# S5 tables of both layers in one opening pass, contiguous weights and a SwiGLU in two halves

## The chip, the cores and the metric

The kernel runs on one core of a Trainium2 chip. The metric is the device time of one execution in microseconds (us). The five engines work side by side, each through its own queue of instructions in program order: TensorE (PE, matmuls; PEld, its weight loads), VectorE (DVE), ScalarE (ACT), GpSimd (POOL) and SyncE (SP), which here issues most transfers. An instruction that waits for a semaphore holds up all that stand behind it on its engine.

## The reference

A trunk of two layers works on 512 tokens, 256 of context and 256 of the latent, of 1024 columns each, in float32. Each layer scales and shifts its input by modulations, projects it, runs four mixers (gated DeltaNet, S5, HGRN2, retention) over it, joins them by an output product with a residual and a layer norm, and ends with a SwiGLU: a dense one of 2816 columns in layer 0, eight experts of 3584 columns, two per token, in layer 1.

```python
for layer in range(DEPTH):
    mod_lat = jax.nn.silu(c) @ ada_w[layer] + ada_b[layer]
    sh1, sc1, gt1, sh2, sc2, gt2 = jnp.split(mod_lat[:, None, :], 6, axis=-1)
    p_lat = _split_proj(_f32((x * (1.0 + sc1) + sh1) @ w_in[layer]))
    ...
    x = _layer_norm(ALPHA * x + gt1 * (mix_lat @ w_out[layer]), ln_g[layer, 0], ln_b[layer, 0])
    # ffn: silu(h @ w1) * (h @ w3) @ w2, dense in layer 0, top 2 of 8 experts in layer 1
    x = _layer_norm(ALPHA * x + gt2 * ffn(x * (1.0 + sc2) + sh2), ln_g[layer, 1], ln_b[layer, 1])

# S5: a diagonal complex state space, per direction, group and state
lam_bar = jnp.exp(lam * jnp.exp(log_step)[..., None])
b_bar = ((lam_bar - 1.0) / lam)[..., None] * lax.complex(b_re, b_im)
h_t = lam_bar * h_(t-1) + b_bar u_t;  y_t = Re(c_mat h_t)
```

The context goes the same way with its own modulations (the last layer needs only the latent's).

## The kernel before

Every product in float32 is made of three matmuls on a high and a low half. `weight` (L340) has SyncE load a block as it is (`wraw`, L344), ACT casts the high half (`whi`, L348) and DVE subtracts the low one (`wlo`, through `tt` at L263). `stationary` and `product` then issue three matmuls of 512 columns per 128 rows (L331): hi with xh, hi with xl, lo with xh, into a PSUM bank `psacc`. A helper's line stands in the profile for all its uses, so tiles tell the stages apart.

`run` puts the stages in this order. (1) `ada` for the first two modulations of layer 0: 16 blocks of 512 KB (`sraw`, 12 buffers), two matmuls each, then a small product `psP`. (2) `first_input` loads the transposed tokens into the same `sraw` ring, scales them and splits them into xh and xl. (3) `mixers(0)`: projections in groups of 256 columns (`w_in`), S5, retention, gated DeltaNet, HGRN2. (4) `mixed`: the output product over the whole of `w_out`, with the residual. (5) `norm_feat`: the layer norm and the modulated input of the SwiGLU. (6) `ffn`: for each of 22 blocks of 128 columns the products with w1 and w3, SiLU times the gate (the multiplication on GpSimd), the high half on ACT and the low half `fgl` on GpSimd; then w2 over 8 output blocks with 22 rows each. (7) a norm that also keeps a transposed copy (`keep`), `mixers(1)`, the output product by tokens, and the experts: 8 experts x 7 steps x 6 units of 1 MB (`mraw`, 8 buffers, L1756).

`s5_tables(l)` prepares what S5 multiplies with. It begins with scalar columns (16 per layer: exponentials, powers of lambda, phases), which DVE and GpSimd compute. Then four groups follow, each with loads of B and C, complex products of 512 columns (`cmul`: the one for the input table `s5W` on DVE with `s5tmp`, the one for the output table on GpSimd with `s5tmq`), 8 transposes of `s5W`, products `s5cz` x `s5W` on TensorE, and writes to DRAM. At the end 16 products with `s5kfb` make a Toeplitz table. Layer 0's tables are called in `mixers(0)` after the first projections, layer 1's between `norm_feat` and `ada(1, ...)`, in a pool of their own.

What stands where on an engine is decided when the program is built: a scheduler lays the instructions of all stages out by priority and by its own estimate of when operands are ready. `prior(off)` and `high_priority(off)` shift a part's priority, contexts name which PSUM banks a part takes, and a pool that isn't left keeps its room. On the chip each engine then keeps that order.

Of the kernel before, what the change touches and what calls it, by code (L numbers as in the profile page):

```python
# [143 lines left out]

def input_arrays(x):
# [14 lines left out]
    for k in ("ada_w", "w_in", "w_out", "ln_g", "ln_b", "ffn_w1", "ffn_w3", "ffn_w2", "moe_w1", "moe_w3", "moe_w2"):  # L160
        arrays[k] = np.ascontiguousarray(g(k))
# [27 lines left out]
class Trunk:  # L189
# [101 lines left out]
    def exp(self, out, x):  # L291

        n = x.shape[1]
        k, r, p = (self.t("ex" + c, [16], bufs=2, pool=self.sc)[:, :n] for c in "krp")
        ki = self.t("exi", [16], I32, bufs=2, pool=self.sc)[:, :n]
# [42 lines left out]
    def weight(self, src, shape, hi_eng="act", lo_eng="vec", pool=None, raw_bufs=3, bufs=2, tag="w", raw=None):  # L338
# [52 lines left out]
    def ada(self, l, part, pool=None, tag="w", bufs=3):  # L391
# [25 lines left out]
    def first_input(self, pool, bufs):  # L417
# [6 lines left out]
        for k0 in range(0, KT, 2):  # L424
            raw = self.t("sraw", [2, NTOK], F32, bufs, pool)
# [17 lines left out]
    def stationary(self, w, xh, xl, acc, eng=("act", "vec")):  # L443

        K = w.shape[1]
        for k0 in range(0, K, 8):
            kn = min(8, K - k0)
            hi, lo = self.weight(w[:, k0:k0 + kn], [kn, P], *eng)
# [7 lines left out]
    def product(self, w, xh, xl, n, fn):  # L456

        for i in range(w.shape[2] // P):
            acc = self.ps("acc")[:, :n]
            self.stationary(w[:, :, i * P:(i + 1) * P], xh, xl, acc)  # L460
            fn(i, acc)

    @projecting
    def proj_feat(self, l, c0, fn, tok=(0, NTOK), ncol=256):

        w = self.A["w_in"][l].rearrange("(k p) f -> p k f", p=P)[:, :, c0:c0 + ncol]
        a, b = tok
# [422 lines left out]
    def gdn_proj(self, l, full):  # L890
# [11 lines left out]
        self.proj_few(l, C_GAB, 16, self.gab)  # L902
# [248 lines left out]
    def s5_tables(self, l):  # L1151
        nc, G = self.nc, self.G
        e = G
        v = lambda k: self.Pm(k).rearrange("p (l g) -> p l g", l=DEPTH)[:, l]
        n = lambda tag, *s: self.t("s5" + tag, list(s))
        self.load_consts("sconsts")
        are, aim = v("s5re"), v("s5im")
        st, ar, ai, t0, t1 = (n(x, 16) for x in ("st", "ar", "ai", "t0", "t1"))
        self.exp(st, v("s5ls"))
# [11 lines left out]
        U = n("u", 2, 16)  # L1171

        h2, sh, ch = (n(x, 16) for x in ("h2", "sh", "ch"))
# [23 lines left out]
        ltmp = n("lt", 16, 4)  # L1197
        pw = lambda a, b: (L[:, 0, :, a:b], L[:, 1, :, a:b])
        for m in (1, 2, 4):
            bc = tuple(x.to_broadcast([P, 16, m]) for x in pw(m, m + 1))  # L1200
            self.cmul(pw(m + 1, 2 * m + 1), pw(1, m + 1), bc, ltmp[:, :, :m])
        self.V.tensor_copy(res[:, 1552:1584].rearrange("p (c g) -> p c g", c=2), L[:, :, :, 8])

        q, nr, den = n("q", 2, 16), n("nr", 16), n("den", 16)
# [14 lines left out]
        LW, LC = n("LW", 2, 16, 8), n("LC", 2, 16, 8)  # L1219
# [13 lines left out]
        pr, pi = self.s5_phases(res)  # L1233
# [798 lines left out]
    def run(self):  # L2032
# [3 lines left out]
        for p in (0, 1):  # L2036
            self.ada(0, p, start, "s", bufs)
# [63 lines left out]
```

## Time and profile before

| | |
|---|---|
| Three runs | 2555.76, 2555.69, 2549.09 us (median 2555.69) |
| Profiled execution | 2555.49 us, span 2553.7 us |
| TensorE busy | 2287.9 us (90%), mean granted clock 0.92 |
| DVE / ACT / GpSimd busy | 1737.5 / 1273.1 / 532.4 us |
| Moved by DMA | 532.76 MB, 209 GB/s over the span |

The stages in the span, by TensorE's instructions: opening up to 70.9 us, mixers of layer 0 to 544.6, w_out to 602.3, norm to 652.5, SwiGLU to about 1030, second norm to 1064, mixers of layer 1 to about 1450, experts to the end. A share of busy time is a mean over stages that are limited by different things, so a stage is read from its own stretch. A matmul is listed with its whole duration although the next one starts before it ends; TensorE's time per matmul is the distance between starts. The granted clock is in tenths of full speed, 1.00 for 2.4 GHz.

### The profile page before, as it was taken

To read this page: it belongs to the slowest core of one execution; us is meant where nothing else is said; L and a number is where in the kernel's file an instruction comes from. 1 tells how busy PE (TensorE), PEld (TensorE's weight loads), DVE (VectorE), ACT (ScalarE), POOL (GpSimd) and SP (SyncE) were. 2 spreads that over 40 slices of the span, in tenths; PEclk is the share of its full clock that TensorE was granted. 3 is DMA by queue.
4 is the path that set the end of the run, shared out by engine and by line. 5 is a ranking of instruction groups with operands and counts; after the bars stand their busy time and mean duration, and the time that the engine had idled before them with its cause. 6 is when DMAs were issued, how large, how long until landed. Compare 5 with 4: busy or idle time off the path is not lost. (4 is left out here: it accounts for less than half of the span.)

```text
span 2553.7 us, 33393 instructions
## 1 busy us (share of the span) xinstructions
PE 2287.9 (90%) x12928; PEld 1790.7 (70%) x12928; DVE 1737.5 (68%) x2352; ACT 1273.1 (50%) x1475; POOL 532.4 (21%) x490
## 2 busy tenths in 40 slices
PE   4979988878899999878896859999999999999997
PEld 1767756554788887447675648878787878788885
DVE  8645636778533322445646689888888888889887
ACT  1542523422544422353533337767676767676774
POOL 4423433327322200333323140000000000001000
PEclk7889987879999999888987869999999999999998
DMA  8343252415533333653230449989898989899994
GB/s 282 115 145 95 80 164 68 153 48 199 153 99 99 97 124 101 213 169 93 64 117 26 146 140 352 371 308 370 308 370 314 363 312 373 316 368 334 370 358 167
DMA packets 338197, 532.76 MB, mean 209 GB/s; under 512 B 32497, under 2 KB 169457, under 8 KB 337649
## 3 DMA queue, kind: packets, MB, share of 16 engines
q1 hardware_dynamic: 312304, 512.79, 58.4%
q10 hardware_dynamic: 25728, 17.77, 2.4%
q8 instruction: 104, 1.70, 0.3%
q14 instruction: 61, 0.49, 0.1%
HBM read 509.23 MB, written 21.28 MB: 208 GB/s over the span
## 5 line engine op out<-in xcount | busy, mean ns | idle before, releaser
L263 DVE TENSOR_TENSOR mlo<-mraw,mhi 128x2048 fp32r<-128x2048 f32 x333 | 769.9, 2325 | 110.2 <-ACT mhi L348 108.6
L348 ACT CAST mhi<-mraw 128x2048 fp32r<-128x2048 f32 x336 | 639.2, 1907 | 215.2 <-PE psh L331 134.0
L331 PE MATMUL psh<-mlo,e_xh 128*128 128x512 f32 x896 | 358.4, 400 | 6.3 <-DVE mlo L263 6.3
L331 PE MATMUL psh<-mhi,e_xh 128*128 128x512 f32 x896 | 351.9, 395 | 13.4 <-ACT mhi L348 7.8
L331 PE MATMUL psh<-mhi,e_xl 128*128 128x512 f32 x896 | 352.1, 393 | 0.0
L348 ACT CAST whi<-wraw 128x1024 fp32r<-128x1024 f32 x142 | 145.7, 1027 | 381.4 <-PE psacc L331 350.8
L331 PE MATMUL psacc<-xh,whi 128*128 128x512 f32 (+2 forms) x784 | 314.1, 402 | 23.7 <-DVE k2P L263 8.1
L263 DVE TENSOR_TENSOR wlo<-wraw,whi 128x1024 fp32r<-128x1024 f32 x142 | 179.6, 1264 | 214.9 <-ACT whi L348 212.6
L331 PE MATMUL psacc<-xh,wlo 128*128 128x512 f32 (+2 forms) x784 | 308.7, 394 | 8.8 <-DVE wlo L263 8.8
L331 PE MATMUL psacc<-xl,whi 128*128 128x512 f32 (+2 forms) x784 | 306.7, 391 | 0.0
L263 POOL TENSOR_TENSOR e_xl<-k2B,e_xh 128x512 fp32r<-128x512 f32 x16 | 31.4, 1968 | 995.9 <-ACT e_xh L1827 995.9
L331 PEld LDWEIGHTS psh<-mhi,e_xh 128*128 128x128 f32 x896 | 170.0, 190 | 52.0 <-ACT mhi L348 8.9
L331 PEld LDWEIGHTS psh<-mlo,e_xh 128*128 128x128 f32 x896 | 170.4, 190 | 43.4 <-DVE mlo L263 8.6
L331 PEld LDWEIGHTS psacc<-xh,whi 128*128 128x128 f32 (+1 forms) x784 | 152.2, 194 | 62.7 <-issue 9.5
L331 PEld LDWEIGHTS psh<-mhi,e_xl 128*128 128x128 f32 x896 | 170.2, 190 | 34.5
L331 PEld LDWEIGHTS psacc<-xh,wlo 128*128 128x128 f32 (+1 forms) x784 | 151.6, 193 | 44.6 <-DVE wlo L263 11.9
L331 PE MATMUL psy<-mlo,e_gh 128*128 128x512 f32 x448 | 176.7, 396 | 0.0
L331 PEld LDWEIGHTS psacc<-xl,whi 128*128 128x128 f32 (+1 forms) x784 | 152.0, 194 | 34.0 <-issue 4.3
L331 PE MATMUL psy<-mhi,e_gl 128*128 128x512 f32 x448 | 173.6, 391 | 0.0
L331 PE MATMUL psy<-mhi,e_gh 128*128 128x512 f32 x448 | 160.0, 394 | 0.0
L331 PEld LDWEIGHTS psy<-mhi,e_gh 128*128 128x128 f32 x448 | 84.3, 188 | 20.0 <-ACT e_gh L1806 1.5
L331 PEld LDWEIGHTS psy<-mhi,e_gl 128*128 128x128 f32 x448 | 84.2, 188 | 18.0
(532 smaller groups left out, 3778.0 us busy)
## 6 DMA issues: line engine op xcount, KB each, us to landing
mraw<-in_moe_w_dram SPq DMA_DIRECT2D x336, 1024.0 KB, 6.3
wraw<-in_ada_w_dram SPq DMA_DIRECT2D x80, 512.0 KB, 4.6
wraw<-in_ffn_w_dram SPq DMA_DIRECT2D x60, 512.0 KB, 3.9
wraw<-in_w_in_dram SPq DMA_DIRECT2D x56, 512.0 KB, 4.0
sraw<-in_ada_w_dram SPq DMA_DIRECT2D x16, 512.0 KB, 9.3
wraw<-in_w_out_dram SPq DMA_DIRECT2D x16, 512.0 KB, 3.6
s5w<-s5wt SPq DMA_DIRECT2D x8, 512.0 KB, 4.8
s5c<-s5W SPq DMA_DIRECT2D x8, 512.0 KB, 4.6
```

What stands on the lines that cost most here:

```text
L263: (eng or self.V).tensor_tensor(out=out, in0=a, in1=b, op=op)
L331: self.T.matmul(out, lhsT, rhs, start=start, stop=stop, **k)
L348: self.S.copy(hi, raw)
```

## The change

On the host, all large weights are laid out anew so that each transfer reads one contiguous block; the transfers stay as many and as large. First the token blocks get their own buffers (`sx`) and the 16 modulation blocks a buffer each. `s5_scalars`, new, computes the scalar columns of both layers in one pass of 32 columns right after `first_input`, and keeps them. `s5_tables` is now only the groups: layer 0's on DVE as before, layer 1's with all their elementwise work on GpSimd, at a shifted priority and beside the SwiGLU. The SwiGLU goes in two halves of 11 blocks, each with its part of w2 (blocks of 8 and 3 rows); the first half's output is kept, gated, in `r`, and the second is added on GpSimd (`ffn_sum`). `norm_feat` and `keep` get rings `lnx` and `lnt` of four buffers instead of the general ring `k2A`.

```diff
+    out["ada_w"] = np.ascontiguousarray(g("ada_w").reshape(DEPTH, KT, P, 6, D).transpose(0, 3, 1, 2, 4))
...
+    moe = np.empty((NE, FE // 512, 6, P, 2048), np.float32)
+    for e in range(NE):
+        for c in range(FE // 512):
+            for j in range(2):
+                for n, w in enumerate((w1, w3)):
+                    moe[e, c, 2 * n + j] = blk(w[e], 4 * j, 4, c * 512, c * 512 + 512).reshape(P, 2048)
+                moe[e, c, 4 + j] = blk(w2[e], 4 * c + 2 * j, 2, 0, D).reshape(P, 2048)
+    out["moe_w"] = moe
...
             raw = self.t(tag + "raw", [n], F32, raw_bufs, pool)
-            self.nc.sync.dma_start(v(raw), src)
+            self.nc.sync.dma_start(raw, src)
...
-        w = self.A["ada_w"][l].rearrange("(k p) f -> p k f", p=P)
         acc = self.ps("acc")
         for k in range(KT):
             raw = self.t(tag + "raw", [1024], F32, bufs, pool or self.wp)
-            self.nc.sync.dma_start(raw, w[:, k, part * D:(part + 1) * D])
+            self.nc.sync.dma_start(raw, self.A["ada_w"][l, part, k])
...
-            raw = self.t("sraw", [2, NTOK], F32, bufs, pool)
+            raw = self.t("sx", [2, NTOK], F32, 4, pool)
             self.nc.sync.dma_start(raw, xt[:, k0:k0 + 2])
...
-    def s5_tables(self, l):
-        nc, G = self.nc, self.G
-        e = G
-        v = lambda k: self.Pm(k).rearrange("p (l g) -> p l g", l=DEPTH)[:, l]
+    def s5_scalars(self, keep):
+
+
+        nc, e = self.nc, self.G
+        NG = DEPTH * 16
         n = lambda tag, *s: self.t("s5" + tag, list(s))
-        self.load_consts("sconsts")
-        are, aim = v("s5re"), v("s5im")
-        st, ar, ai, t0, t1 = (n(x, 16) for x in ("st", "ar", "ai", "t0", "t1"))
-        self.exp(st, v("s5ls"))
+        are, aim = self.Pm("s5re"), self.Pm("s5im")
+        st, ar, ai, t0, t1 = (n(x, NG) for x in ("st", "ar", "ai", "t0", "t1"))
+        self.exp(st, self.Pm("s5ls"))
...
-        LW, LC = n("LW", 2, 16, 8), n("LC", 2, 16, 8)
+        LW, LC = (self.t("s5L" + x, [2, NG, 8], pool=keep) for x in "WC")
...
+        self.s5r = [self.dr.tile([P, 1584], F32, name=f"s5r{l}") for l in range(DEPTH)]
+        for l in range(DEPTH):
+            nc.sync.dma_start(self.s5r[l], res[:, l])
+        self.s5k = q, LW, LC
+
+    def s5_tables(self, l, eng):
+
+        nc, e = self.nc, self.G
+        n = lambda tag, *s: self.t("s5" + tag, list(s))
+        self.load_consts("sconsts")
+        f, b = slice(0, 64), slice(64, P)
+        q, LW, LC = (v[:, :, 16 * l:16 * l + 16] for v in self.s5k)
         dt = lambda tag, *sh: self.dr.tile(list(sh), F32, name=f"s5{tag}{l}")
...
-            self.ts(Cm[:, 2], Cm[:, 1], -1.0, ALU.mult)
+            self.ts(Cm[:, 2], Cm[:, 1], -1.0, ALU.mult, eng=eng)
             qb = tuple(q[:, c, gs, None].to_broadcast([P, 4, 16]) for c in range(2))
-            self.cmul((bb[:, 0], bb[:, 1]), (B[:, 0], B[:, 1]), qb, bb[:, 2])
+            self.cmul((bb[:, 0], bb[:, 1]), (B[:, 0], B[:, 1]), qb, bb[:, 2], eng=eng)
...
-            self.cmul((Wv[:, 0], Wv[:, 1]), lw, wb, tmp)
+            self.cmul((Wv[:, 0], Wv[:, 1]), lw, wb, tmp, eng=eng)
...
-                self.V.tensor_copy(cz[rows, :, d], Cm[rows, ::2])
+                self.ts(cz[rows, :, d], Cm[rows, ::2], 1.0, ALU.mult, eng=eng)
...
-            x = self.s2()
+            x = self.t("lnx", [NTOK], bufs=4)
...
     def ffn(self, l, xt, r):
+
         A = self.A
-        NF = FF // P
-        w1, w3, w2 = (A[k][0].rearrange("(k p) f -> p k f", p=P) for k in ("ffn_w1", "ffn_w3", "ffn_w2"))
-        gs = [[self.t(f"fg{c}{j}", [NF // 2, NTOK], F32R) for c in "hl"] for j in range(2)]
-        gh, gl = ([gs[f // (NF // 2)][c][:, f % (NF // 2)] for f in range(NF)] for c in range(2))
-        for f in range(NF):
-            h = self.s2()
-            sl = slice(f * P, f * P + P)
-            self.product(w1[:, :, sl], self.xh, self.xl, NTOK, lambda i, acc: self.silu(h, acc, self.s2()))
-            self.product(w3[:, :, sl], self.xh, self.xl, NTOK, lambda i, acc: self.mul(h, h, acc))
-            self.S.copy(gh[f], h)
-            self.sub(gl[f], h, gh[f].bitcast(F32), eng=self.G)
-        res = self.big.tile([P, KT, NTOK], F32, tag="xl", name=self.name("fres"))
-        self.load_res(res, xt, (0, 1))
-        pm = self.ps()
-        self.product(w2, gh, gl, NTOK, lambda i, acc: self.residual(r, res, i, acc, pm, l, 5))
+        NF, NH = FF // P, FF // P // 2
+        res = pm = None
+        for j in range(2):
+            gh, gl = (self.t(f"fg{c}", [NH, NTOK], F32R) for c in "hl")
+            for n in range(NH):
+                h, f = self.s2(), j * NH + n
+                self.product([[A["ffn_w1"][f]]], self.xh, self.xl, NTOK, lambda i, acc: self.silu(h, acc, self.s2()))
+                self.product([[A["ffn_w3"][f]]], self.xh, self.xl, NTOK, lambda i, acc: self.mul(h, h, acc))
+                self.S.copy(gh[:, n], h)
+                self.sub(gl[:, n], h, gh.bitcast(F32)[:, n], eng=self.G)
+            if j == 1:
+                res = self.big.tile([P, KT, NTOK], F32, tag="xl", name=self.name("fres"))
+                self.load_res(res, xt, (0, 1))
+                pm = self.ps()
+            w2 = [[A["ffn_w2"][i, P * P * k0:P * P * (k0 + kn)].rearrange("(p f) -> p f", p=P)
+                   for k0, kn in ((j * NH, 8), (j * NH + 8, NH - 8))] for i in range(KT)]
+            self.product(w2, gh, gl, NTOK, lambda i, acc: self.ffn_sum(r, res, i, acc, pm, l))
         return pm
+
+    @prior(-300)
+    def ffn_sum(self, r, res, i, acc, pm, l):
+
+        t = r[:, i] if res is None else self.s2()
+        for s in range(2):
+            sl = slice(s * 256, s * 256 + 256)
+            self.act(t[:, sl], acc[:, sl], AF.Copy, scale=self.mod(l, 5, s)[:, i:i + 1])
+        if res is None:
+            return
+        self.add(r[:, i], r[:, i], t, eng=self.G)
+        self.stt(r[:, i], res[:, i], ALPHA, r[:, i], ALU.mult, ALU.add)
+        self.mm(pm, self.ones[:, :P], r[:, i], start=(i == 0), stop=(i == KT - 1))
...
-        start, bufs = self.enter("start", "right"), 12
+        start = self.enter("start", "right")
         for p in (0, 1):
-            self.ada(0, p, start, "s", bufs)
-        self.first_input(start, bufs)
+            self.ada(0, p, start, "s", 16)
+        self.first_input(start)
         self.leave("start")
+        keep = self.enter("s5k", "left")
+        self.enter("s5s", "left")
+        self.s5_scalars(keep)
+        self.leave("s5s")
         self.mixers(0, None, {"gdn": (2, 3), "end": (4, 5)})
         xt1 = self.dr.tile([P, KT, NTOK], F32, name="xt1")
         self.enter("l0", "left")
...
         self.norm_feat(r, pm, 0, 0, 3, 0,
                        lambda k, x: self.nc.scalar.dma_start(xt1[:, k], x))
         self.leave("l0")
-        self.enter("tab", "right")
-        with self.context("B"):
-            tables = self.s5_tables(1)
-        self.leave("tab")
         for p in (0, 1):
             self.ada(1, p)
         self.enter("l1", "right")
         r = self.t("lr", [KT, NTOK])
+
+        self.enter("tab", "left")
+        with self.context("B"), self.tc.high_priority(-2000):
+            tables = self.s5_tables(1, self.G)
         self.enter("f0", "left")
         pm = self.ffn(0, xt1, r)
-        self.leave("f0")
-        self.mx = self.open["l1"][1]
+        self.leave("f0", "tab", "s5k")
+        self.enter("l1n", "left")
         for p in (4, 5):
             self.ada(1, p)
         self.xtok = self.dr.tile([P, 2, D], F32, name="xtok")
 
         def keep(k, x):
 
-            pt, t = self.ps(), self.s2()
+            pt, t = self.ps(), self.t("lnt", [256], bufs=4)
             for j in range(2):
                 self.T.transpose(pt[:, j * P:(j + 1) * P], x[:, 256 + j * P:256 + (j + 1) * P], self.ident)
-            self.act(t[:, :256], pt[:, :256], AF.Copy)
-            self.nc.scalar.dma_start(self.xtok[:, :, k * P:(k + 1) * P], t[:, :256].rearrange("p (j x) -> p j x", j=2))
+            self.act(t, pt[:, :256], AF.Copy)
+            self.nc.scalar.dma_start(self.xtok[:, :, k * P:(k + 1) * P], t.rearrange("p (j x) -> p j x", j=2))
         self.norm_feat(r, pm, 0, 1, 0, 1, keep)
-        self.leave("l1")
+        self.leave("l1n", "l1")
```

In the queue of TensorE at the opening, rows before; `sraw` are the modulation weights, `s5W` and `s5cz` tables, `xh`, `whi` the first projection:

```order
15 L331 MATMUL psacc_154<-sraw_175,csk 32x512 x2
16 L1278 MATMUL psA_937<-consts_74,s5W_927 128x128 x4
17 L331 MATMUL psacc_154<-sraw_179,csk 32x512 x2
18 L1278 MATMUL psA_943<-consts_74,s5W_927 128x128 x4
19 L331 MATMUL psA_952<-s5cz_911,s5W_927 128x2x16 x7
20 L331 MATMUL psacc_154<-sraw_183,csk 32x512 x2
21 L331 MATMUL psA_952<-s5cz_911,s5W_927 128x2x16
22 L331 MATMUL psP_189<-consts_74,k2P_187 128x4 x4
23 L1278 MATMUL psA_994<-consts_74,s5W_984 128x128 x4
24 L1278 MATMUL psA_1000<-consts_74,s5W_984 128x128 x4
25 L331 MATMUL psA_1009<-s5cz_911,s5W_984 128x2x16 x8
26 L331 MATMUL psacc_247<-xh_195,whi_251 128x512
```

and in the changed kernel:

```order
15 L373 MATMUL psacc_154<-sraw_175,csk 32x512 x2
16 L373 MATMUL psacc_154<-sraw_179,csk 32x512 x2
17 L373 MATMUL psacc_154<-sraw_183,csk 32x512 x2
18 L373 MATMUL psP_189<-consts_74,k2P_187 128x4 x4
19 L373 MATMUL psacc_468<-xh_195,whi_472 128x512
20 L373 MATMUL psacc_468<-xl_196,whi_472 128x512
21 L373 MATMUL psacc_502<-xh_195,whi_506 128x512
```

The last two pairs of modulation matmuls and `psP_189` moved ahead of all S5 matmuls, and projections follow at once.

In DVE's queue, the last table group of layer 0; `wlo` are low halves of projection weights, `k2P` and `kq` belong to the gated DeltaNet. Before:

```order
264 L263 TENSOR_TENSOR s5W_1041<-s5W_1041,s5tmp_1042 128x4x8x16
265 L263 TENSOR_TENSOR s5tmp_1099<-s5LW_824,s5bb_1086 128x512
266 L279 TENSOR_SCALAR s5C_1085<-s5C_1085 128x64
267 L263 TENSOR_TENSOR s5W_1098<-s5LW_824,s5bb_1086 128x4x8x16 x2
268 L1283 COPY s5cz_911<-s5C_1085 64x2x64 x2
269 L263 TENSOR_TENSOR wlo_320<-wraw_318,whi_321 128x1024
270 L263 TENSOR_TENSOR s5W_1098<-s5W_1098,s5tmp_1099 128x4x8x16
271 L263 TENSOR_TENSOR s5tmp_1099<-s5LW_824,s5bb_1086 128x512
272 L263 TENSOR_TENSOR s5W_1098<-s5W_1098,s5tmp_1099 128x4x8x16
```

and now:

```order
278 L305 TENSOR_TENSOR s5tmp_1053<-s5LW_376,s5bb_1040 128x512
279 L305 TENSOR_TENSOR s5W_1052<-s5W_1052,s5tmp_1053 128x4x8x16
280 L305 TENSOR_TENSOR s5tmp_1110<-s5LW_376,s5bb_1097 128x512
281 L305 TENSOR_TENSOR wlo_811<-wraw_809,whi_812 128x128
282 L305 TENSOR_TENSOR s5W_1109<-s5LW_376,s5bb_1097 128x4x8x16 x2
283 L305 TENSOR_TENSOR s5W_1109<-s5W_1109,s5tmp_1110 128x4x8x16
284 L321 TENSOR_SCALAR s5cz_922<-s5C_1096 64x2x64 x2
285 L305 TENSOR_TENSOR kq_536<-k2P_616,k2P_620 128x512
286 L305 TENSOR_TENSOR s5tmp_1110<-s5LW_376,s5bb_1097 128x512
287 L305 TENSOR_TENSOR s5W_1109<-s5W_1109,s5tmp_1110 128x4x8x16
288 L317 SCALAR_TENSOR_TENSOR k2P_710<-psacc_679,params,k2P_710 128x2x255 x2
```

Low halves and the DeltaNet's work, which stood behind the last `s5W`, now stand ahead of it and among its instructions.

In GpSimd's queue inside the SwiGLU; each step has the SiLU product (`k2A`) and the low half `fgl`. Before:

```order
229 L263 TENSOR_TENSOR lr_4444<-lr_4444,lnrs_4771 128x512 x5
230 L263 TENSOR_TENSOR k2A_5468<-k2A_5468,k2A_5500 128x512
231 L263 TENSOR_TENSOR fgl_878_5465<-k2A_5468,fgh_877_5464 128x512
232 L263 TENSOR_TENSOR k2A_5540<-k2A_5540,k2A_5572 128x512
233 L263 TENSOR_TENSOR fgl_878_5465<-k2A_5540,fgh_877_5464 128x512
234 L263 TENSOR_TENSOR k2A_5612<-k2A_5612,k2A_5644 128x512
```

and now, about the sixth step of the first half:

```order
233 L305 TENSOR_TENSOR k2A_5626<-k2A_5626,k2A_5658 128x512
234 L305 TENSOR_TENSOR fgl_5265<-k2A_5626,fgh_5264 128x512
235 L305 TENSOR_TENSOR k2A_5698<-k2A_5698,k2A_5730 128x512
236 L321 TENSOR_SCALAR s5cz_4991<-s5C_5051 64x2x64 x2
237 L305 TENSOR_TENSOR s5W_5099<-s5LC_377,s5C_5051 128x4x8x16 x2
238 L305 TENSOR_TENSOR fgl_5265<-k2A_5698,fgh_5264 128x512
239 L305 TENSOR_TENSOR s5W_5099<-s5W_5099,s5tmq_5066 128x4x8x16
240 L305 TENSOR_TENSOR s5tmq_5066<-s5LC_377,s5C_5051 128x512
241 L305 TENSOR_TENSOR s5W_5099<-s5W_5099,s5tmq_5066 128x4x8x16
242 L305 TENSOR_TENSOR k2A_5770<-k2A_5770,k2A_5802 128x512
243 L305 TENSOR_TENSOR s5tmq_5123<-s5LC_377,s5C_5108 128x512
244 L321 TENSOR_SCALAR s5C_5165<-s5C_5165 128x64
```

Table instructions of layer 1 (`s5cz`, `s5W`, `s5tmq`) now stand between the two instructions of a step and between steps.

## Rows read from the trace of the kernel before

**Rows 1.** Stretches: busy us by engine, granted clock, DMA share, GB/s.

```profile
core 0: us, PE busy (x) PEld busy (x) DVE busy (x) ACT busy (x) POOL busy (x), PEclk, DMA share, GB/s
0.00:64.00 64.00, 27.20 (x108) 10.88 (x108) 52.02 (x242) 6.68 (x12) 31.62 (x49) 0.75 0.81 281
64.00:128.00 64.00, 57.64 (x256) 47.73 (x255) 43.93 (x66) 37.47 (x76) 31.21 (x23) 0.85 0.36 115
704.00:768.00 64.00, 64.00 (x285) 52.97 (x284) 22.98 (x24) 27.86 (x36) 17.88 (x12) 1.00 0.32 93
1728.00:1792.00 64.00, 64.00 (x287) 52.62 (x286) 57.40 (x33) 47.37 (x32) 3.25 (x2) 1.00 1.00 366
```

**Rows 2.** Waits of SyncE's queue: total us, times, longest.

```profile
SPq L1756 <- DVE mlo L263: 850.7, 325, 14.2
SPq L344 <- DVE wlo L263: 582.8, 106, 18.0
```

**Rows 3.** Timeline of TensorE, opening: start us, duration, operation, wait.

```profile
41.66 1.11 PE L1278 MATMUL psA<-consts,s5W 128*128 128x128 f32 x4 [11.03 <-DVE s5W L263]
...
62.99 1.09 PE L1278 MATMUL psA<-consts,s5W 128*128 128x128 f32 x4 [8.07 <-DVE s5W L263]
...
70.92 1.20 PE L331 MATMUL psacc<-xh,whi 128*128 128x512 f32 x2
```

**Rows 4.** Timeline of TensorE around S5's products; last, s5U's load issue.

```profile
139.03 0.39 PE L331 MATMUL psacc<-xh,wlo 128*128 128x512 f32 x1
...
152.32 3.65 PE L331 MATMUL psA<-s5U,s5tabwc 128*128 128x64 f32 x16 [12.04 <-DMA s5U<-s5u]
...
163.23 3.68 PE L331 MATMUL psA<-s5U,s5tabwc 128*128 128x64 f32 x32
...
172.39 1.89 PE L331 MATMUL psA<-s5U,s5tabwc 128*128 128x64 f32 x16
...
L1343 ACTq DMA_DIRECT2D s5U<-s5u x2: 366/805/1244, 132.8 to 133.2; - x2
```

**Rows 5.** Timeline of DVE, last table groups of layer 0.

```profile
79.32 1.17 DVE L263 TENSOR_TENSOR s5W<-s5W,s5tmp 128x512 f32<-128x512 f32 x1
...
95.26 1.24 DVE L263 TENSOR_TENSOR s5W<-s5W,s5tmp 128x512 f32<-128x512 f32 x1
```

**Rows 6.** DVE by form, 30 to 64: count | busy, mean ns | idle.

```profile
L263 DVE TENSOR_TENSOR s5W<-s5W,s5tmp 128x512 f32<-128x512 f32 x3 | 6.0, 1995 | 0.0
```

**Rows 7.** Stretches as rows 1: w_out, first norm, second norm.

```profile
544.60:602.30 57.70, 53.13 (x210) 39.98 (x214) 52.69 (x210) 13.77 (x25) 32.04 (x39) 0.89 0.29 94
602.30:652.50 50.20, 40.33 (x188) 20.82 (x187) 44.09 (x64) 19.12 (x42) 30.97 (x23) 0.94 0.74 249
1030.20:1064.30 34.10, 25.91 (x83) 7.46 (x83) 20.77 (x52) 14.63 (x30) 15.26 (x6) 0.82 0.83 268
```

**Rows 8.** TensorE by form, 570 to 680, table matmuls.

```profile
L331 PE MATMUL psB<-s5kfb,sconsts 128*128 128x256 f32 x32 | 10.9, 509 | 7.1 <-ACT s5wt L287 4.5 <-ACT s5kfb L287 2.6
L331 PE MATMUL psB<-s5cz,s5W 128*128 128x32 f32 x64 | 7.7, 271 | 0.0
L1278 PE MATMUL psB<-consts,s5W 128*128 128x128 f32 x32 | 5.1, 277 | 0.0
```

**Rows 9.** Waits of TensorE, 544 to 720.

```profile
PE psacc L331 <- DVE wlo L263: 5.0, 3, 4.1
```

**Rows 10.** Waits of TensorE, 1064 to 1110, the kept copy.

```profile
PE psA L2067 <- ACT k2A L285: 7.7, 3, 2.9
```

**Rows 11.** GpSimd and DVE by form, 704 to 768, in the SwiGLU.

```profile
L263 POOL TENSOR_TENSOR fgl<-k2A,fgh 128x512 fp32r<-128x512 f32 x6 | 10.5, 1752 | 16.0 <-ACT fgh L1633 16.0
L263 POOL TENSOR_TENSOR k2A<-k2A,k2A 128x512 f32<-128x512 f32 x6 | 7.7, 1290 | 31.0 <-ACT k2A L287 31.0
...
L263 DVE TENSOR_TENSOR wlo<-wraw,whi 128x1024 fp32r<-128x1024 f32 x12 | 14.7, 1225 | 1.6 <-ACT whi L348 1.0
```

**Rows 12.** GpSimd by form, 576 to 680, a table instruction.

```profile
L263 POOL TENSOR_TENSOR s5W<-s5W,s5tmq 128x512 f32<-128x512 f32 x7 | 11.8, 1692 | 0.2
```

More of the change, by code (lines that the diff above doesn't have):

```diff
@@ L159, in input_arrays @@
     }
-    for k in ("ada_w", "w_in", "w_out", "ln_g", "ln_b", "ffn_w1", "ffn_w3", "ffn_w2", "moe_w1", "moe_w3", "moe_w2"):
+    arrays |= weight_arrays(x)
+    for k in ("ln_g", "ln_b"):
         arrays[k] = np.ascontiguousarray(g(k))
@@ L440, in new_xm, with stationary @@
         self.xl = self.big.tile([P, KT, NTOK], F32R, tag="xl", name=self.name("xl"))
[L443 to L448, printed above, removed]
+    def stationary(self, blocks, xh, xl, acc, eng=("act", "vec")):
+        K = sum(b.shape[1] for b in blocks) // P
+        for k0, src in zip(range(0, K, 8), blocks):
+            kn = src.shape[1] // P
+            hi, lo = self.weight(src, [kn, P], *eng)
             for k in range(kn):
@@ L1575, in mixed @@
         self.load_res(res, src, (0, 1))
-        w = self.A["w_out"][l].rearrange("(k p) f -> p k f", p=P)
+        w = [[self.A["w_out0"][i]] for i in range(KT)]
         pm = self.ps()
@@ L1590, in out_part @@
     def out_part(self, l, ks, last=None):
-        w = self.A["w_out"][l].rearrange("(k p) f -> p k f", p=P)
         for k in ks:
-            hi, lo = self.weight(w[:, k], [D])
+            hi, lo = self.weight(self.A["w_out1"][k], [D])
             for b in range(2):
@@ L1808, in down @@
         for j0 in range(0, 4, 2):
[L1809 removed]
+            hi, lo = self.unit(w(c, 4 + j0 // 2), 2)
             for j in range(2):
@@ L1856, in experts @@
         steps = [(n, c) for n in range(len(jobs)) for c in range(NC)]
-        early = [self.unit(src, 4, "pool") for src in self.up_srcs(*jobs[0][:2], 0)[:3]]
-        parts = self.up_parts(*jobs[0][:2], 0, 3)
+        early = [self.unit(src, 4, "pool") for src in self.up_srcs(jobs[0][0], 0)[:3]]
+        parts = self.up_parts(jobs[0][0], 0, 3)
         self.ex, self.exi = [None, None], 0
-        x = {0: self.gather(jobs[0][3])}
+        x = {0: self.gather(jobs[0][1])}
         y, g, back = {}, {}, None
@@ L1911, in moe @@
         self.enter("m", "left")
-        self.experts([self.expert(e) + [[self.pos[:, j, e:e + 1] for j in range(2)],
-                                               lambda e=e: [self.rG[:, j, e:e + 1] for j in range(2)]]
-                      for e in range(NE)], True)
+        self.experts([(self.expert(e), [self.pos[:, j, e:e + 1] for j in range(2)],
+                       lambda e=e: [self.rG[:, j, e:e + 1] for j in range(2)]) for e in range(NE)], True)
         n = nc.values_load(self.nover[0:1, 0:1], min_val=0, max_val=3)
@@ L1962, in mixers @@
             self.enter("tab", "left")
-            tables = self.s5_tables(l)
+            tables = self.s5_tables(l, self.V)
             self.leave("tab")
```

132 lines of the change are left out of this document (76 added, 56 removed).

## Prediction

> **What bounds the kernel now.** I read the table by stretches of 64 us first, since the mean of 90% for TensorE hides very unequal stages. In the SwiGLU (704 to 768) and inside an expert (1728 to 1792) TensorE is busy for 64.00 of 64 us at granted clock 1.00, with 285 and 287 matmul records [rows 1]: 64.00/285 = 0.2246 us for each matmul of 512 columns, the unit of everything below. There only fewer or cheaper matmuls help, and any matmul added costs its full time. The first 64 us are the opposite: TensorE 27.20, DVE 52.02, clock 0.75 [rows 1]. Then I asked what SyncE's queue waits for: it waits for DVE's low halves to free a raw buffer, 850.7 us in the experts and 582.8 us in the trunk [rows 2]. So weights arrive too early, not too late.
>
> The timeline of TensorE in the opening shows the queue in program order doing harm: the last modulation matmuls stand behind transposes of S5 tables, and TensorE waits 11.03 and 8.07 us for DVE's s5W; the first projection matmul starts at 70.92 [rows 3]. Later it waits 12.04 us for s5U [rows 4]. Around the first norm, w_out takes 57.7 us and the norm 50.2 us, with DVE at 52.69 and 44.09 and GpSimd at 32.04 and 30.97 busy; the same norm after the SwiGLU takes 34.1 us [rows 7].
>
> **The change part by part.** Durations come from the profiled execution: 2555.49 us with a span of 2553.7, and 0.2 us from the median of 2555.69. The sum is made against 2555.5.
>
> *A, the opening.* All 32 modulation matmuls and both small products now precede 72 projection matmuls, and these precede the first S5 transpose. Before, the wait of 11.03 us began at 41.66 - 11.03 = 30.6 [rows 3]; without it the last matmuls and the small product end near 35; about 5 us for scaling and splitting the input put the first projection near 40 instead of 70.92. That is not all gain, for DVE takes over as the bound: it now has the low halves of ten weight blocks (1.23 us each [rows 11], 12 us) between the table groups, and the last s5W subtraction, which started at 95.26 before [rows 5], comes at about 95 + 12 = 108. Before, 192 projection matmuls were done by 139.03 + 0.39, S5's products ran from 152.32 to 172.39 + 1.89 = 174.3 among further projections, and the 262nd projection was done 31 matmuls later, at 181; without the S5 products themselves (3.65 + 3.68 + 1.89 = 9.2 us) that is 172 [rows 4]. After, from 108, the last group's transposes and products, 24 projections and the products of kfb take at most 1.3 + 1.9 + 5.4 + 10.9 = 19.5 us [rows 8], 17 with some overlap, and the load of s5U, issued only then, 19.5 us (152.32 - 132.8 [rows 4]): S5's products begin at 144, and in the new order 262 projections stand before them. Gain 172 - 144 = 28. Bounds: if DVE doesn't bind, TensorE's own work from 40 on (192 x 0.2246 = 43, 30 of tables, of kfb and of small products, then the load) gives 132 and a gain of 40; if the 24 wide table instructions of DVE stay at the stretched 1995 ns instead of 1.17 us [rows 5, 6], up to 24 x 0.8 = 20 us more go and some 12 remain. I take 28, nearer to the row of the stretched opening.
>
> *B, w_out and the first norm.* The 192 matmuls of w_out need 192 x 0.2246 = 43.1 us and took 57.7 [rows 7]; of the difference nearly 5 us went for low halves behind table work (5.0 up to 720 [rows 9]), and a quarter of the table matmuls stood between. I take -8 (-3 to -11). The norm without tables beside it is the second one, 34.1 against 50.2 us: -16 (-8 to -18). The kept copy waited 7.7 us for ACT's k2A, in three pieces [rows 10], and gets rings of its own: -6 (0 to -8).
>
> *C, the same table matmuls inside the SwiGLU.* Between 570 and 680, before, 32 transposes, 64 small products and 32 of kfb were 5.1 + 7.7 + 10.9 = 23.7 us busy [rows 8]; successive ones may overlap as the projections do (0.39 us listed [rows 4], one every 0.2246), so between 12 and 24, and I take the middle, +18. They stand between psacc matmuls in a stage that has no idle time, so nothing hides them.
>
> *D, GpSimd beside the SwiGLU.* In the first half (11 steps of 48 x 0.2246 = 10.78 us, 264 matmuls of w2 and C: 118.6 + 59.3 + 18 = 196 us) GpSimd already has the SiLU multiplication and the subtraction, 1290 + 1752 ns per step [rows 11], 33 us. The tables bring 48 instructions of 512 columns, between DVE's 1.17 us [rows 5] and 1.69 [rows 12] each, and 36 narrow ones, taken at 0.3 to 0.5: 70 to 100 us. So it fits on average, 133 of 196 at the upper end. But queued behind a waiting table instruction on GpSimd stand the next SiLU product and the next fgl; for the first DVE's product with psacc waits, and so a PSUM bank; behind a late s5W the psacc matmuls wait, since TensorE's queue is in order too. The scheduler has put the table instructions where they fit, so most of it is covered by 10.78 us per step; if that cover is gone, every us over it is lost. I take +8 (0 to 45).
>
> What the rows say of the two engines together: the same subtraction took 1.17 us at 79.32, when GpSimd had been idle for a while, and 1995 ns on average between 30 and 64, when GpSimd worked beside it [rows 5, 6]; in the SwiGLU the low half takes 1225 ns with GpSimd busy for 18 of 64 us [rows 1, 11], so how it fares beside a full GpSimd is not in this trace. The Trainium skill, "SBUF — State Buffer", section "Who interferes with whom", says that a VectorE instruction with two SBUF inputs and a GpSimd instruction that reads SBUF contend for one interface, and that whoever comes second waits for the whole instruction of the other. The stretch in the opening agrees with it (1995 against 1170 ns). By that rule each of the two low halves of a step can hold up a table instruction for its 1.23 us, and if half of that reached TensorE, D would be 8 + 11 x 2.46 x 0.5 = 22 and the time 2541.
>
> *E, the SwiGLU's second product in short blocks.* 16 blocks hold 3 instead of 6 or 8 rows: 9 matmuls, 2.0 us, against at most 1.23 us for the low half [rows 11]; only a block that comes before its operands costs. The extra gated sum on GpSimd (8 additions) follows in the second half. +4 (0 to 8).
>
> *F, contiguous weights.* SyncE waits for buffers, not for bytes [rows 2], and TensorE is full [rows 1]: 0 in the trunk and 0 in the experts. The scalar columns of both layers at once double the width of instructions of 16 columns, not their number: 0 to +2, inside A.
>
> Sum: -28 - 8 - 16 - 6 + 18 + 8 + 4 = -28, so 2527 us.
>
> **The rivals.**
> *The opening stays bound by DVE.* For it: 52.02 of 64 us busy [rows 1]; against it: DVE is idle for 20 of the next 64. The lower bound of A, 12, gives a sum of -12 and 2544.
> *GpSimd gates the steps, and the kernel ends slower.* The place is the first 11 steps: if every table instruction takes half as long again (1.7 to 2.5 us, 150 us in all) and three quarters of them fall there, GpSimd has 33 + 113 = 146 us of work against 118.6, 27 too many, and TensorE, in order, loses about as much again at the transposes of the four groups: D is 52 instead of 8, and the time 2555.5 - 36 + 52 = 2571. It decides from D = 44 on, where the time passes 2563, the bound of slower. For it: the stretch of rows 5 and 6 and the queue of two kinds of work on one engine; against it: DVE is busy for only 22.98 of 64 us there [rows 1]. It is what the rule named under D would bring at its fullest.
> *The experts speed up.* For it: DMA share 1.00 at 366 GB/s [rows 1]; against it: the wait of 850.7 us for buffers [rows 2]. If the stretches at an expert's change shorten by 3 us at each of seven changes, 2527 - 21 = 2506.
> *The change does not do what it says:* the gain of the opening is given back later in layer 0, where the recurrent mixers wait for each other and not for projections: A falls to 0 and the time to 2555.
>
> **How the numbers follow.** Forecast 0.52 (its own range 2505 to 2546), opening bound by DVE 0.20, GpSimd gating 0.14, experts faster 0.06, given back 0.08. What can be told from no change is 0.3%, 7.7 us: under 2548 is faster, over 2563 slower. Faster: 0.52 + 0.06 + two thirds of 0.20 = 0.71; same: a third of 0.20 and most of 0.08 = 0.12; slower: 0.14 and the rest = 0.17. Range: from the experts' case with the bounds of B, 2490, to the lower half of the GpSimd case, 2565.
>
> **What would show it.** A: first projection near 40, and S5's products at 132 to 160. B: w_out near 49 us and the norm near 34. C and D: TensorE still full between 704 and 900 with table matmuls among psacc, idle under 10 us; POOL near 60% busy. F: 0.2246 and 0.223 us per matmul, 366 GB/s and the wait for buffers unchanged. The prediction is wrong if TensorE waits for s5W or s5cz by more than 40 us in the SwiGLU, if the opening gives under 10, or if the experts' stretch changes by over 10 us.

## The result, and the profile after

The changed kernel takes 2591.90 us in the median (2586.84 to 2599.65, 4 runs) beside 2555.73 (2549.09 to 2559.80) of the kernel before: ratio 1.0162, interval 1.0137 to 1.0186. It is 36 us slower; 2527 was predicted, between 2490 and 2565. The profiled execution took 2587.91 us with a span of 2586.1, which is 32.4 more than the 2553.7 before.

The stages in us, from TensorE's first matmul of one stage to the first of the next. The last column is experiment e9 below, the change without its two overlaps in memory. The second norm is taken here from the end of the SwiGLU's matmuls (1026.0 before), 4.2 us earlier than in [rows 7].

| stage | before | after | difference | predicted | e9 |
|---|---|---|---|---|---|
| start to w_out | 544.6 | 590.9 | +46.3 | A: -28 | 534.5 |
| w_out and first norm | 107.8 | 79.7 | -28.1 | B: -24 | 78.9 |
| SwiGLU | 373.6 | 391.9 | +18.3 | C, D, E: +30 | 391.8 |
| second norm, kept copy | 38.3 | 42.9 | +4.6 | B: -6 | 43.8 |
| layer 1 to the experts | 450.5 | 442.0 | -8.5 | 0 | 442.6 |
| experts and end | 1038.9 | 1038.7 | -0.2 | 0 | 1038.5 |

Everything from w_out on together gives -14, where +0 was predicted. The loss is all in the first row. In both kernels this stretch holds 3360 matmuls; before, and then after:

```profile
0.00:544.60 544.60, 439.43 (x3360) 322.10 (x3360) 329.67 (x776) 196.78 (x373) 199.22 (x220) 0.85 0.41 130
0.00:590.90 590.90, 459.26 (x3360) 334.94 (x3360) 347.78 (x777) 197.02 (x373) 206.66 (x219) 0.81 0.36 120
```

TensorE's idle time grows from 105.2 to 131.6 us, by 26; its busy time for the same matmuls grows by 20, at a lower granted clock. These are shorter stretches of after; the columns are those of [rows 1], and the first two and the fifth answer to rows there:

```profile
0.00:64.00 64.00, 33.50 (x136) 16.93 (x137) 51.29 (x260) 18.64 (x35) 18.24 (x38) 0.84 0.80 296
64.00:128.00 64.00, 43.33 (x193) 34.99 (x191) 57.86 (x63) 23.45 (x43) 42.07 (x31) 0.79 0.30 104
224.00:256.00 32.00, 18.70 (x108) 17.59 (x106) 6.43 (x8) 2.36 (x5) 1.65 (x2) 0.68 0.45 123
256.00:288.00 32.00, 22.86 (x71) 13.41 (x71) 11.45 (x21) 13.00 (x21) 12.51 (x15) 0.61 0.05 17
704.00:768.00 64.00, 63.45 (x292) 52.38 (x291) 26.63 (x23) 27.66 (x38) 50.66 (x48) 1.00 0.32 108
```

DVE is no freer in the opening than before, and between 224 and 288 TensorE works for only 41.56 of 64 us, at clocks of 0.68 and 0.61. The timelines of TensorE, DVE and TensorE again (start, duration, operation, in brackets the wait) answer to [rows 3 to 5]:

```profile
45.58 0.79 PE L373 MATMUL psacc<-xh,whi 128*128 128x512 f32 x1 [14.30 <-ACT whi L390]
...
72.94 1.11 PE L1328 MATMUL psA<-consts,s5W 128*128 128x128 f32 x4 [5.14 <-DVE s5W L305]
```
```profile
60.55 0.49 DVE L305 TENSOR_TENSOR s5bb<-s5B,s5q 128x64 f32<-128x64 f32 x3
...
131.64 1.81 DVE L305 TENSOR_TENSOR s5W<-s5W,s5tmp 128x512 f32<-128x512 f32 x1
```
```profile
177.45 3.68 PE L373 MATMUL psA<-s5U,s5tabwc 128*128 128x64 f32 x32
...
261.18 6.16 PE L373 MATMUL psA<-s5yt,s5glu 128*128 128x256 f32 x16 [15.12 <-DVE s5yt L305]
```

The first projection came 25 us earlier, as forecast in kind, but the first table instruction of DVE (s5bb) starts at 60.55 instead of 29.81, the last subtraction at 131.64 instead of 95.26, and S5's products at 177.45 instead of 152.32. The timeline of SyncE shows why s5bb is late, before and then after:

```profile
1.18 14.73 SPq L399 DMA_DIRECT2D sraw<-in_ada_w_dram  x12
16.71 0.33 SPq L1263 DMA_DIRECT2D s5B<-in_s_b_re_dram  x1
```
```profile
24.55 2.89 SPq L386 DMA_DIRECT2D wraw<-in_w_feat_dram  x3
48.15 0.81 SPq L1293 DMA_DIRECT2D s5r<-s5res  x2
49.88 1.65 SPq L386 DMA_DIRECT2D wraw<-in_w_feat_dram  x2
51.59 0.84 SPq L1313 DMA_DIRECT2D s5B<-in_s_b_re_dram  x1
```

The tables' small loads now stand behind the input, three weights and the stores of s5r, and these waited 19.7 us for DVE's s5res. Before, the same loads stood between the modulation blocks, the first at 16.71. Nothing in the diff moves these loads: the scheduler did, and the question for the experiments was what made it.

### The profile page after: what moved, and what is told of

The parts are those of the page before. It is cut to its first block, busy times and chain, and to the rows that moved or that the text cites. A ratio compares the mean times of both kernels' runs of the same rounds, so it can differ in the third digit from the quotient of the medians.

```text
span 2586.1 us, 33270 instructions
## 1 busy us (share of the span) xinstructions
PE 2301.8 (89%) x12928; PEld 1795.7 (69%) x12928; DVE 1702.9 (66%) x2151; ACT 1279.7 (49%) x1499; POOL 574.9 (22%) x528
## 5 line engine op out<-in xcount | busy, mean ns | idle before, releaser
L390 ACT CAST whi<-wraw 128x1024 fp32r<-128x1024 f32 (+1 forms) x150 | 147.0, 982 | 409.4 <-PE psacc L373 373.6
L305 DVE TENSOR_TENSOR wlo<-wraw,whi 128x1024 fp32r<-128x1024 f32 (+1 forms) x150 | 193.3, 1292 | 227.7 <-ACT whi L390 207.2
L373 PE MATMUL psacc<-xl,whi 128*128 128x512 f32 (+2 forms) x784 | 312.0, 398 | 0.8 <-DVE xl L317 0.8
```

The costliest lines, as they stand in the source:

```text
L305: (eng or self.V).tensor_tensor(out=out, in0=a, in1=b, op=op)
L373: self.T.matmul(out, lhsT, rhs, start=start, stop=stop, **k)
L390: self.S.copy(hi, raw)
```

## The experiments

The addresses of the buffers in the two built programs gave a theory, in bytes of one partition:

```
                       first tables      start pool        last s5yt          zf begins
before                 up to 171008      from 180192       181184 to 183232   183744
after                  128128 to 163968  from 147424       186048 to 188096   183744
```

*M:* the start pool of 80 KB lies over the first tables' working buffers (s5W, s5tmp, s5tmq and s5wt, over modulation blocks), and the scalars' scratch (as far as 133728) lies over the tables' constants; so the tables cannot begin before the modulations and the scalars are done. *K* (formed after the first four runs): the kept pool of 4352 bytes, and 512 more for the wider scratch of exp, push S5's last buffer, which had ended 512 bytes below the retention gate's zf, over zf; so the retention must wait for S5's end. The rivals: *D*, *W*: VectorE's pass over 32 columns and the earlier low halves cost the time; *R*: the moved tables cost something later.

**M taken away, in two ways.** e8 uses one ring for the modulations and the input and puts the scalars' scratch (`s5s`) apart, so that neither overlap is left:

```diff
-            raw = self.t("sx", [2, NTOK], F32, 4, pool)
+            raw = self.t("sraw", [2, NTOK], F32, 11, pool)
...
+        self.enter("s5s", "right")
+        s5s = self.open["s5s"][1]
...
-            self.ada(0, p, start, "s", 16)
+            self.ada(0, p, start, "s", 11)
```

> The changed kernel with the pass over both layers' scalars early, as it has it, but with the scratch in memory of its own until the tables are done, and tokens and modulation weights in one ring of 11 buffers, so that nothing of layer 0's tables lies over anything earlier. Theory M: as the run with late scalars, about 2540 (2530 to 2550), S5's products near 150. Theory D: the early pass still stands ahead of the first groups; S5's products after 165 and 2570 to 2590.

e1 has the same ring and computes the scalars in the tables' own pool, behind the first projections in program order.

> The changed kernel with two things taken back in the opening: the modulation weights and the tokens share one ring again (of 11 buffers), and the scalar columns of both layers are computed where layer 0's tables are, in their pool. The first weights of S5's groups (s5B, s5C) then stand in SyncE's queue after the twelfth modulation block, as before the change. Theory M (memory: layer 0's table pool lies over the 16 + 4 buffers and the scalars' scratch, so its loads come after them, S5 starts some 25 us late, and layer 0 loses 46): S5's first products near 150, w_out from about 545, the whole about 2540 (2532 to 2550), with the norm and SwiGLU as in the changed kernel. Theory D (DVE: pass of 32 columns and low halves ahead of the tables make the opening late by themselves): S5's products after 165 and the time over 2565.

Measured: e8 2577.05 us (ratio 1.0096, 1.0074 to 1.0118) and e1 2579.26 (1.0116, 1.0090 to 1.0142), both far above the 2540 that was expected by M. S5's products came back from 177.5 to 143.7 and 157.7, so M is the cause of their delay; D is not: e8 has the early pass, and though the times lie where D had forecast them, its late products did not come. But w_out still began at 575.5 and 581.1: M was not all.

**M alone, and the layout alone, added to the kernel before.** e3 gives the kernel before 16 + 4 start buffers and nothing else.

> The kernel before with one edit: 16 buffers for the modulation blocks and four of their own for the tokens (80 KB instead of 48 per partition), so that layer 0's table pool lies over them. Nothing else of the change is in it. Theory M: S5's loads come after the first five projection blocks, the first projection near 42, but S5's products near 175 and the time 2580 to 2605. Theory D: no pass of 32 columns, so the earlier projections are a gain: 2525 to 2550.

x4 is the kernel before with the contiguous weights and nothing else; the order of the work is unchanged.

> The kernel before with the contiguous layout of all large weights alone; order of instructions on all engines as before. If transfers are hidden everywhere, as the prediction has it: within 0.3% of before (2548 to 2563), experts unchanged. If the experts were bound by transfers: 2525 to 2545, shorter between 1515 and the end.

e3: 2590.29 us (1.0154, 1.0132 to 1.0176). Eight more buffers, with no instruction added, cost as much as the whole change. The tables' first load moved from 16.71 to 42.12, behind five weights, and S5's first product to 177.5:

```profile
23.98 18.09 SPq L344 DMA_DIRECT2D wraw<-in_w_in_dram  x5
42.12 3.79 SPq L1263 DMA_DIRECT2D s5B<-in_s_b_re_dram  x1
```

x4: 2547.13 (0.9983, 0.9966 to 1.0000): nothing that can be told.

**The change without its opening, with and without a pool of 4 KB.** y1 keeps 16 columns and the ring of 12 in the opening, and computes the second layer's scalars and tables beside the halved SwiGLU. v1 is y1 with a pool that nothing uses:

```diff
+        self.enter("s5k", "left")
+        self.t("dummyk", [1088])
         self.mixers(0, None, {"gdn": (2, 3), "end": (4, 5)})
...
-        self.leave("f0", "tab")
+        self.leave("f0", "tab", "s5k")
```

> The change without its opening: the scalars of 16 columns, the ring of 12 and the 48 KB start pool stand as before; the second layer's scalars are computed beside the SwiGLU together with its tables, whose groups are on GpSimd; the SwiGLU in two halves, the norms' own buffers and the contiguous weights stay. Theory K (all that the change lost came from memory that it takes in the first layer): the output projection starts as before, at 545 +- 8 us, then the projection, the norm, the SwiGLU and the second norm measure as in the changed kernel (-13.5, -14.6, +18.3, +4.6): 2547 - 5 = 2542, between 2530 and 2552, ratio 0.990 to 0.999. Rival R (the halved SwiGLU and the moved tables cost something later, in layer 1's mixers or the experts): 2560 or more.

> The kernel of the run above with one thing more: a pool of 4352 bytes that nothing uses, held on the left from layer 0's mixers to the SwiGLU's end, as the change holds the kept columns. No instruction is added. Theory K: the pool pushes the last S5 buffers (s5yt, which ended 512 bytes below the retention gate's zf) over zf, so the retention's products stand behind S5's end: they start some 30 us later, the output projection starts 15 to 30 us later than in the run above, and the time is 2555 to 2575. Rival W (what was left of the loss is VectorE's pass over 32 columns): no more than 3 us from the run above.

y1: 2540.73 us (0.9957, 0.9941 to 0.9973). The total met what was expected in part by luck: the SwiGLU took 403.1 us instead of the changed kernel's 391.9, and shorter stages behind it made up for that (second norm 37.9 instead of 42.9, layer 1 439.9 instead of the 450.5 of before). v1: 2575.14 (1.0088, 1.0063 to 1.0113). An empty pool of 4352 bytes costs 34 us; w_out begins at 572.9 instead of 539.4. In v1 the last s5yt lies at 185536 to 187584, over zf. Stretches of TensorE, y1 and then v1 (columns as above):

```profile
224.00:256.00 32.00, 32.00 (x153) 23.76 (x154) 17.71 (x26) 14.60 (x24) 11.51 (x13) 1.00 0.35 99
256.00:288.00 32.00, 32.00 (x152) 21.66 (x149) 16.79 (x24) 17.29 (x28) 8.74 (x11) 1.00 0.22 75
```
```profile
224.00:256.00 32.00, 21.67 (x79) 15.17 (x78) 15.68 (x25) 12.66 (x20) 8.61 (x8) 0.84 0.38 107
256.00:288.00 32.00, 32.00 (x113) 20.29 (x114) 6.92 (x9) 12.18 (x19) 7.79 (x10) 0.73 0.08 25
```

and the retention's first product against S5's glu, y1 and then v1:

```profile
220.57 1.95 PE L373 MATMUL psP<-ra,rv 128*64 128x256 f32 x16
...
247.13 1.02 PE L373 MATMUL psA<-s5yt,s5glu 128*128 128x256 f32 x4
```
```profile
241.12 6.05 PE L373 MATMUL psA<-s5yt,s5glu 128*128 128x256 f32 x16 [6.08 <-DVE s5yt L305]
...
256.87 1.12 PE L373 MATMUL psP<-ra,rv 128*64 128x256 f32 x2
```

In y1 the retention fills the time before S5's glu; in v1 its products stand behind it, TensorE has nothing to put in front, and the granted clock is 0.84 and 0.73 where it was 1.00. TensorE's sequence up to 199 us is the same in both. DVE's timeline shows the buffers themselves, y1 and then v1:

```profile
234.35 0.68 DVE L321 TENSOR_SCALAR zf<-psacc 128x512 f32<-128x512 f32 x1
...
258.51 1.09 DVE L305 TENSOR_TENSOR k2A<-k2A,s5yt 128x256 f32<-128x256 f32 x2
```
```profile
250.97 1.09 DVE L305 TENSOR_TENSOR k2A<-k2A,s5yt 128x256 f32<-128x256 f32 x2 [1.86 <-ACT k2A L329]
253.17 1.27 DVE L321 TENSOR_SCALAR zf<-psacc 128x512 f32<-128x512 f32 x2
```

In y1 zf is first written while s5yt is still in use; in v1 only after the last read of s5yt, and in the changed kernel too (273.3, with the last reads from 271.1 on). That the pool moves the retention this way is shown. But it moves all other buffers on the left by as much, and some of the gated DeltaNet's now lie over others of the retention's; how much of the 34 us is zf's alone was not tested.

**Both overlaps taken away.** e9 is e8 with q, LW and LC stored to DRAM and loaded again beside the SwiGLU, so that no pool is kept (s5yt ends at 183744, where zf begins):

```diff
+        self.s5kd = self.dr.tile([P, 1088], F32, name="s5kd")
+        nc.sync.dma_start(self.s5kd, kt)
...
-        keep = self.enter("s5k", "left")
```

> The change with its scalars of 32 columns at the opening, in scratch that overlaps nothing (as in the run with the scratch apart, ring of 11), but q, LW and LC go to DRAM and are loaded again for the second tables, so that no pool of 4352 bytes is kept through layer 0. Theory K: the retention starts before S5's end again, the output projection starts at 545 to 556 instead of 575.5, 2540 to 2556. Rival W (32 columns on VectorE cost the rest): the output projection still starts after 570, 2570 to 2580.

2532.87 us (0.9914, 0.9892 to 0.9937): 44 us under e8, 20 under the kernel before, the fastest of all and below the 2540 to 2556 expected, with the 32 columns still at the opening. W falls. Its retention starts in front of S5's glu again, and its stages stand in the table above.

```profile
153.07 3.68 PE L373 MATMUL psA<-s5U,s5tabwc 128*128 128x64 f32 x32
...
233.31 1.95 PE L373 MATMUL psP<-ra,rv 128*64 128x256 f32 x16
```

**K alone taken away.** w1 is the changed kernel with only the kept values in DRAM.

> The changed kernel, whole, with one thing undone: q, LW and LC go to DRAM and are loaded again for the second tables, so that no pool is kept through layer 0; the start pool of 80 KB and the scalars' scratch still lie under the first tables' buffers, so the tables' loads still stand behind the layer's first input. Theory M+K (two losses of their own): the first S5 product at 177 +- 8 us as in the changed kernel, the retention ahead of S5's end again, the output projection at 550 to 562 (556 where the same order of TensorE's work ran with the first layer's 16 columns only), the time 2540 to 2565. If the two overlaps don't add (the kept pool mattered only with an early S5): 2580 to 2595.

2574.71 us (1.0061, 1.0031 to 1.0091), outside what was expected by M+K and by its rival. S5's first product came at 180.6 and the retention was in front again, but w_out began at 577.3; this profile is of the longest of ten runs, which lay between 2550 and 2585. Either overlap by itself leaves most of the loss: from 2592, M's removal gives 15 and K's 17; the second removal then gives 42 to 44.

**M alone, again.** The runs of e3 had lain at 2564 once and at 2590 to 2592 four times.

> The kernel before with 16 + 4 start buffers, a second time: its runs lay at 2563.87 once and at 2590 to 2592.5 four times, and the profile was of the one at 2563.87. Theory M: the order of work is fixed, so the runs differ in the granted clock alone (0.924 and 0.910 to 0.914 over the span), and a profile at 2590 shows the same chain with longer stretches at 1.2 GHz. Rival: a transfer lands later in the longer runs, and a wait that the short one doesn't have appears in the opening.

2589.79 us (1.0134, 1.0103 to 1.0166), profiled at 2598.72. Here the same program at 2564 and at 2599 can be laid side by side, first the profile of the former:

```profile
192.00:224.00 32.00, 30.55 (x175) 24.67 (x175) 28.10 (x27) 9.49 (x16) 21.93 (x11) 1.00 0.18 54
224.00:256.00 32.00, 29.74 (x173) 21.66 (x172) 10.86 (x14) 5.27 (x11) 2.68 (x4) 1.00 0.34 94
```
```profile
192.00:224.00 32.00, 30.58 (x180) 24.90 (x179) 27.77 (x29) 9.99 (x18) 21.16 (x11) 1.00 0.23 73
224.00:256.00 32.00, 30.32 (x97) 20.17 (x97) 11.07 (x12) 3.68 (x8) 3.67 (x3) 0.58 0.26 76
256.00:288.00 32.00, 32.00 (x113) 24.19 (x114) 7.26 (x11) 8.06 (x13) 1.95 (x4) 0.62 0.30 73
```

TensorE is busy for about the same time, but in the second the granted clock is 0.58 and 0.62, near the lower level of 1.2 GHz, and 97 matmuls are recorded where there were 173. Waiting does not explain it: up to w_out TensorE's idle time is 113.6 us in the longer run, against 117.6 in the shorter. So M costs some 10 us by waits, and some 30 more in the runs that get the lower clock. w1's spread fits that (clock 0.929 and 0.926 over the span at 2554 and 2550, 0.917 at 2585), but no second profile shows it.

**Waits and clock apart.** Up to w_out all these kernels have 3360 or 3361 matmuls, so TensorE's time splits into idle time and busy time of the same work, in us, one profile each:

| kernel | w_out begins | busy | idle |
|---|---|---|---|
| before | 544.6 | 439.4 | 105.2 |
| after (M and K) | 590.9 | 459.3 | 131.6 |
| w1 (M) | 577.3 | 456.5 | 120.8 |
| K: e8, e1 | 575.5, 581.1 | 455.7, 459.7 | 119.8, 121.4 |
| e9 (neither) | 534.5 | 430.9 | 103.6 |
| before with M: e3, e3 again | 556.1, 582.0 | 438.5, 468.4 | 117.6, 113.6 |
| y1, and with K: v1 | 539.4, 572.9 | 436.4, 451.0 | 103.0, 121.9 |

Against e9, M alone adds 17 us of idle time, K alone 16 to 18, both 28: the waits nearly add. The busy time grows by 26, by 25 to 29, and by 28: in these profiles either overlap by itself already brings the lower clock, and the second adds little, so one removal gave little. For K, e1's profile shows it in the shortest of its runs; w1's is of its longest, and in e3's shorter run M alone came without it.

**The tables' groups on DVE.** y2 is y1 with `self.s5_tables(1, self.V)`.

> As the first run of these, with the second tables' groups on VectorE instead of GpSimd. In the changed kernel GpSimd was busy for 50 of 64 us beside the SwiGLU and TensorE idled for 4.6 us in all of it. If GpSimd's long operations cost nothing there: the same time within 3 us. If they stretch VectorE's (the prediction's term of +8): 5 to 10 us faster than with GpSimd. If VectorE becomes late with the low halves: slower by 5 to 20.

2544.10 us (0.9971, 0.9954 to 0.9987): no difference from y1 that can be told in the whole. In the stage itself there is one: the SwiGLU took 411.0 us against y1's 403.1, with TensorE idle for 15.9 against 11.1, and a layer 0 that was 7.4 us shorter hides it. One profile of each does not say more, but VectorE is not the better place.

## Why the prediction was wrong, step by step

**A failed, -28 against +46, and it failed as a reading of the order.** The step counted instructions on DVE and TensorE and took from the new order that 262 projections would stand before S5's products; "S5's products begin at 144" then rested on the ten low halves on DVE (12 us) alone. The 262 were right, but the products began at 177.45, since the tables had to wait for memory: the step did not ask why the loads and table groups had moved behind the input. By its own measure, which puts the kernel before at 172, that is 5.5 us lost instead of 28 gained. The other 41 of the 46.3 us are lost behind S5's products, where the step took layer 0 to follow unchanged: the kept pool cost nothing in the sum and 34 us in v1, and no term stood for the lower clock.

Two numbers agree by luck. e8 has S5's products at 143.7, the forecast's number, but with 168 projections before them and the first of these at 59.8 instead of 40. And e9 stands at 2532.87, within 6 us of the forecast, because A's -10 instead of -28 meets a SwiGLU of +18 instead of +30 and a layer 1 that was not forecast. Even with both overlaps gone the opening gains little: w_out starts at 534.5 in e9, and in kernels with the opening of before at 544.6 (before), 533.9 (x4), 539.4 (y1) and 532.0 (y2), which differ by up to 8 us in TensorE's busy time and 4.5 in its idle time. The 32 columns pay elsewhere: y1, which computes the second scalars beside the SwiGLU, needs 403.1 us for it, e9 391.8.

**B was right in sum for w_out and the first norm** (-13.6 for w_out, more than its range of -3 to -11, and -14.5 for the norm, predicted -8 and -16). The kept copy's -6 cannot be read from the row of the second norm, which took 4.6 us longer: before, most of the copy's transposes and its waits of 7.7 us stood behind layer 1's first projection [rows 10], so in the next row, and now most stand in front of it. The waits themselves fell from 7.7 to 3.6 us, part of what was forecast. Second norm and layer 1 together are 3.9 us shorter.

**C was right, D and E too high.** Before, TensorE was busy for 370.84 of the SwiGLU's 373.6 us; after, the same stage reads:

```profile
670.60:1062.50 391.90, 387.31 (x1724) 317.21 (x1725) 136.47 (x148) 153.85 (x236) 162.70 (x140) 0.99 0.36 116
```

The table matmuls add 387.31 - 370.84 = 16.5 us (predicted 18), and idle time grows from 2.8 to 4.6: 1.8 for D and E, predicted 12. GpSimd is busy for 50.66 of the 64 us from 704 on and for 53% up to 896, near the forecast's 60%. In the first of these stretches the low halves do take longer, 1706 ns instead of the 1225 of [rows 11]:

```profile
L305 DVE TENSOR_TENSOR wlo<-wraw,whi 128x1024 fp32r<-128x1024 f32 x11 | 18.8, 1706 | 9.0 <-ACT whi L390 8.8
```

That is what the Trainium skill, "SBUF — State Buffer", "Who interferes with whom", says of two engines at one interface, and the trace agrees with it in direction. The size does not follow GpSimd's busy time alone: in y2 the low half took 1500 ns with GpSimd busy for 25.83 of the same 64 us. DVE had 37 of 64 us to spare, and in the whole stage TensorE waited 2.2 us for low halves, 0.4 before. The rival "GpSimd gates the steps" is dead: it needs 44 us or more of D, and TensorE idles for 4.6 us in all of the stage.

**F was right**: x4, and the experts at 1038.7 us against 1038.9 with 331 GB/s in both. Of the rivals, "given back" named the right place, layer 0 behind the opening, but for another reason and not far enough. Not predicted was layer 1, 8.5 us shorter. Part of it is the kept copy's waits; a wait of TensorE of 15.38 us for S5's s5H, at 1142 before, has no like in after, but another, for the gated DeltaNet's gXs, grew from 10.6 to 18.0, and the idle time of the whole row fell by only 3.6. What brings the rest was not tested. The lower end of the range, 2490, does not come out of the terms it names: 2506 less the 7 us by which B's bounds go below B is 2499. Nothing hangs on it.

Open is why the clock falls in M's order in some runs and holds in others.

## What to carry to other kernels

When a change enlarges, adds or keeps a buffer, compare the addresses first: here a pool of 4 KB moved a whole branch, since a buffer had only 512 bytes to spare, and the sum over moved instructions did not show it. When the new order puts work somewhere that the diff doesn't explain, find the buffer that forbids the old place before pricing the new one. To test it, add an unused pool of the same size to a kernel that hasn't the change, or send the kept values through DRAM. When two removals do not add, split the engine's time into idle and busy: waits and clock can behave differently.

## What the runs showed of the hardware

The same program, with the same order of work, ran with a span of 2562.1 and of 2597.0 us: after 32 us at clock 1.00 with TensorE busy for 30.55 and 30.58, the clock of the next 32 us was 1.00 in one and 0.58 in the other. VectorE's low half took 1225 ns beside a GpSimd busy for 18 of 64 us and 1706 ns beside one busy for 51. The contiguous weight layout alone (x4) changed neither the experts' 331 GB/s nor the time that can be told, but the DMA engines moved these bytes in a busy share of 0.88 instead of 0.92.
